# Feed-forward by block products: own buffers for the weights back, two weight sums in place, and 1/rms after the first plain products

## The chip, the cores and the metric

One Trainium2 chip, one core of it. The time is the device time of one execution in microseconds (us), the median of several runs. Below, "the trace" is the record of one profiled execution; all instants in it are us from the start of its span.

The engines are named as in the profile: PE is the matrix engine, DVE the vector engine, ACT the scalar engine, POOL the GpSimd engine, SP the engine that issues most loads. SBUF is the memory on the chip, PSUM the banks that PE writes into.

## What is computed

The program runs two blocks of two layers each, over 512 tokens of width 1024. The change concerns the feed-forward part of the second block alone, which is called once in each of its two layers (l = 0, 1):

```
def rms_norm_2(x, g): ...          # x / sqrt(mean(x*x) + eps) * g
def conv_glu_ffn(x, w_up, conv_w, conv_b, w_down):
    h = x @ w_up                                   # 1024 -> 2 * 2816
    a, b = h[..., :D_FF], h[..., D_FF:]
    ap = jnp.pad(a, ((0, 0), (CONV_WIDTH - 1, 0), (0, 0)))
    conv = conv_b + ap[:, 0:S] * conv_w[0]
    for j in range(1, CONV_WIDTH):
        conv = conv + ap[:, j:j + S] * conv_w[j]
    return (jax.nn.silu(conv) * b) @ w_down        # 2816 -> 1024
...
    x = x + conv_glu_ffn(rms_norm_2(x, norm2_g), w_up, conv_w, conv_b, w_down)
```

After the last layer the result is normalised once more (`final_norm_g`).

## The kernel before

**Layout.** x lies transposed: 8 tiles `x[k]` of 128 features by 512 tokens. Every fp32 product is made of three fp32r products: a number is split into a rounded part `hi` and a rest `lo` (on ACT a cast, on DVE a subtraction), and hi·hi + hi·lo + lo·hi is summed in PSUM. All matmuls have one line, L165; the tiles' names tell them apart. The weights come in pieces of 1 MB (`w_up`, 8 x 256 columns) or 0.5 MB (`w_down`, 4 x 256).

**Buffers.** A tile is taken by a tag and a number of buffers; a tile that is taken when all buffers of its tag are in use waits until the oldest is free. `raw()` (L249) has two buffers in the pool `wp`, and so have `whi` and `wlo`, the two parts of a split weight. `wget` loads into `raw` and splits at once (ACT L261, DVE L262). Before, `w_up` and `w_down` both go through `wget` or the same tag, so their pieces take the two `raw` buffers in turn.

**Feed-forward, `ffn2` (L1860).** The 22 tiles of hidden features are 11 pairs, each pair with a half `a` (convolved, then silu: `conv`) and a half `b` (`gate`). The first two pairs (`NPLAIN`), so four calls of `up`, are plain products: `plain` (L1777) multiplies 8 k-tiles by the two halves of the tokens, 96 matmuls of 256 columns each call. The other nine pairs go by block products, `strassen` (L1827): a 2 by 2 block product in the Winograd form with seven products of 12 matmuls of 256 columns, 84 in all. One such call, here a **step**, yields two tiles of 128 features. There are 18 steps a layer, 36 in all. Its seven weight operands come from `strassen_weights` (L1790): three are blocks of the weight itself (split on ACT L1798 and DVE L1799), four are sums of blocks, made on POOL (L1804 to L1807, s3, s1, s2, s4, into `sraw`) and split by ACT L1809 and DVE L1810 into `shi`, `slo`. The operands on the other side are blocks of h (`ha`, `hb`) and four sums of them (`ht`).

The products with `w_down` of the chunk of pairs before (24 matmuls of 512 columns, `down`) follow one to a step, two to a step in the last chunk. The last of the seven products is put off behind them (`settle`).

**The start of it.** At the end of the mixer ahead, `rms` (L325 on) makes for each half of the tokens the sum of squares (ACT L337, DVE and POOL L339), sums it over the partitions by a matmul into `n`, and takes 1/rms from it by ACT L393 and a Newton step on DVE (L394 to L396), into `r`. Only then does `halved` make h = x·gain·r, split, half of the tiles by POOL L1726 and ACT L1728, half by DVE L1734. A generator, `sums`, adds the four token sums of one k after every plain call: POOL L1747 (x·r, twice), ACT L1749, POOL L1755 to L1758, and splits.

**The end of it.** The last two tiles' product runs segment by segment, followed by the next norm or, in the last layer, by `last_rows` (L1970), which writes the result out.

**Order.** Nothing here is ordered by hand. A scheduler with a model of the engines' times puts all instructions of an engine in one fixed order; each engine works its list off in that order, and waits where an operand or a buffer isn't there yet.

Of the kernel before, what the change touches and what calls it, by code (L numbers as in the profile page):

```python
# [8 lines left out]
F32 = mybir.dt.float32  # L9
F32R = mybir.dt.float32r  # L10
I32 = mybir.dt.int32
AF = mybir.ActivationFunctionType
# [4 lines left out]
P = 128  # L17
# [132 lines left out]
class Kern:  # L150
# [1553 lines left out]
    def halved(self, x, r, scale, bias, fp, gtag, gbufs):  # L1704
# [4 lines left out]
        B = [[[None] * 4 for _ in range(2)] for _ in range(2)]  # L1709
        for k in range(KD):  # L1710
            j, kk = k // 4, k % 4
            hs = [self.t(fp, [P, S if j else H], F32R, "hb" if j else "ha", 8) for _ in range(2)]
            B[j][0][kk] = [h[:, 0:H] for h in hs]
            if j:
                B[1][1][kk] = [h[:, H:S] for h in hs]
            else:
                both = self.t(fp, [P, S], F32R, gtag, gbufs)
                B[0][1][kk] = [both[:, 0:H], both[:, H:S]]
        T = [[self.t(fp, [P, 4, H], F32R, "ht", 8) for _ in range(2)] for _ in range(4)]
        for n in range(2):  # L1720
            c = slice(n * H, (n + 1) * H)
            for k in range(KD):
                hi, lo = B[k // 4][n][k % 4]
                v = self.small(H)
                if k % 2:
                    nc.gpsimd.tensor_tensor(v, x[k][:, c], r[:, c], op=OP.mult)  # L1726
                    if bias is None:
                        nc.scalar.activation(v, v, AF.Copy, scale=scale(k))  # L1728
                    else:
                        nc.scalar.activation(v, v, AF.Identity, scale=scale(k), bias=bias(k))  # L1730
                    nc.scalar.copy(hi, v)
                    nc.vector.tensor_tensor(lo, v, hi.bitcast(F32), op=OP.subtract)
                else:
                    nc.vector.scalar_tensor_tensor(v, x[k][:, c], scale(k), r[:, c], op0=OP.mult, op1=OP.mult)  # L1734
                    if bias is None:
                        nc.scalar.copy(hi, v)
                        nc.vector.tensor_tensor(lo, v, hi.bitcast(F32), op=OP.subtract)
                    else:
                        nc.scalar.activation(hi, v, AF.Identity, bias=bias(k))
                        nc.vector.scalar_tensor_tensor(lo, v, bias(k), hi.bitcast(F32), op0=OP.add, op1=OP.subtract)  # L1740

        def sums():
            for kk in range(4):
                u = []
                for k in (kk, kk + 4):
                    u.append(self.tmp(S))
                    nc.gpsimd.tensor_tensor(u[-1], x[k], r, op=OP.mult)  # L1747
                    if bias is None:
                        nc.scalar.activation(u[-1], u[-1], AF.Copy, scale=scale(k))  # L1749
                    else:  # L1750
                        nc.scalar.activation(u[-1], u[-1], AF.Identity, scale=scale(k), bias=bias(k))
# [7 lines left out]
                hi, lo = T[kk]  # L1759
# [8 lines left out]
        return B, T, sums()  # L1768

    def strassen_setup(self, B, T, fp):  # L1770
        self.sB, self.sT = B, T
        self.sraw = self.t(fp, [P, 4, 512], F32, "sraw", 1)
        self.shi = self.t(fp, [P, 5, 512], F32R, "shi", 1)
        self.slo = self.t(fp, [P, 5, 512], F32R, "slo", 1)
        self.fp, self.owed, self.odd = fp, None, 0

    def plain(self, ws, n=2):  # L1777
# [12 lines left out]
    def strassen_weights(self, ap2d, c0):  # L1790
# [269 lines left out]
```

## Time and profile before

| | |
|---|---|
| median of 3 runs | 3638.54 us (3634.24 to 3639.56) |
| the profiled execution | 3637.94 us, its span 3636.2 us |
| granted PE clock, mean | 0.979 of full |
| PE busy | 3435.1 us, 94% |
| DVE busy | 2501.4 us, 69% |
| ACT busy | 1483.0 us, 41% |
| POOL busy | 1038.3 us, 29% |
| loads from memory | 120 GB/s over the span |

Busy shares are means over the whole program. The feed-forward of the second block begins at 2537 in layer 0 and at 3230 in layer 1; its two starts and the steps inside it are looked at by themselves below.

### The profile page before, as it was taken

Reading aid. Unit: us, or ns where it says so; the run is one execution under the profiler, and the core shown is the slowest. Engines: PE = TensorE matmul, PEld = TensorE weight load, DVE = VectorE, ACT = ScalarE, POOL = GpSimd, SP = SyncE. Lnnn points to the kernel's source line nnn. Section 1 sums busy time; section 2 is a strip of 40 time slices with the busy share of each in tenths; the row PEclk is TensorE's granted clock in tenths of the full one; section 3 lists DMA queues with packets and bytes.
Section 4 is the critical chain, followed back from the end, with each engine's and each line's share of the span. In section 5 each row is a group of like instructions: output and inputs, shape, how many; then the busy total and the mean of one; then the engine's idle time right before and its main releaser. Section 6 shows DMA issues by size and latency. Waiting matters only on the chain.

```text
span 3636.2 us, 51011 instructions
## 1 busy us (share of the span) xinstructions
PE 3435.1 (94%) x19782; PEld 2929.3 (81%) x19782; DVE 2501.4 (69%) x4093; ACT 1483.0 (41%) x2377; POOL 1038.3 (29%) x976
## 2 busy tenths in 40 slices
PE   7998999999999989999999999989999999989998
PEld 5887788888888878878887887766888877769887
DVE  5457866468786675565767557896867769787666
ACT  4233544242222243365443333335543443454444
POOL 2242322310000023212311003652534227444441
PEclk9999999999999999999999999999999999999999
DMA  6377553413333324754423324352132352513222
GB/s 220 117 238 185 145 134 107 138 59 118 104 120 112 110 95 131 240 129 130 143 87 120 122 81 127 111 166 78 57 103 88 96 160 82 174 36 99 94 87 85
DMA packets 358610, 438.79 MB, mean 121 GB/s; under 512 B 41343, under 2 KB 310289, under 8 KB 358369
## 3 DMA queue, kind: packets, MB, share of 16 engines
q1 hardware_dynamic: 327648, 345.48, 31.8%
q0 software_dynamic: 19200, 71.17, 5.6%
q10 hardware_dynamic: 11520, 18.89, 1.7%
q8 instruction: 156, 2.56, 0.3%
q14 instruction: 86, 0.70, 0.1%
HBM read 363.78 MB, written 71.70 MB: 120 GB/s over the span
## 4 chain that ended last, share of the span: by engine, by line
PE 51%; DVE 13%; DMA 5%; issue 4%; POOL 4%; ACT 2%; SPq 0%; DVEq 0%; ACTq 0%; POOLq 0%
PE d L165 25%; PE s L165 18%; PE n L165 4%; DMA raw<-in__w_up 3%; POOL sraw L1807 2%; DVE wlo L262 1%; DVE wlo L1799 1%; POOL sraw L1805 1%; PE o L165 1%; DVE sc L1394 1%; POOL sraw L1806 1%; PE g L165 1%; DVE m L1393 1%; ACT shi L1809 1%; PE d L178 1%
## 5 line engine op out<-in xcount | busy, mean ns | idle before, releaser
L261 ACT CAST whi<-raw 128x2048 fp32r<-128x2048 f32 (+2 forms) x235 | 353.4, 1504 | 487.6 <-PE s L165 247.3
L165 PE MATMUL s<-h,whi 128*128 128x256 f32 (+3 forms) x2176 | 528.6, 335 | 12.3 <-ACT whi L261 6.5
L262 DVE TENSOR_TENSOR wlo<-raw,whi 128x2048 fp32r<-128x2048 f32 (+2 forms) x219 | 405.4, 1851 | 182.8 <-ACT whi L261 182.0
L165 PE MATMUL d<-h,whi 128*128 128x512 f32 (+2 forms) x1456 | 451.8, 392 | 16.4 <-DVE h L1272 6.1
L165 PEld LDWEIGHTS s<-h,whi 128*128 128x128 f32 (+1 forms) x2176 | 370.9, 190 | 59.0 <-ACT whi L261 6.8
L165 PE MATMUL d<-g,whi 128*128 128x512 f32 (+1 forms) x1328 | 369.2, 365 | 6.1 <-DVE x L1071 2.3
L165 PE MATMUL s<-h,wlo 128*128 128x256 f32 (+3 forms) x1088 | 362.2, 334 | 2.3 <-DVE wlo L262 2.3
L165 PEld LDWEIGHTS d<-h,whi 128*128 128x128 f32 (+1 forms) x1456 | 272.1, 192 | 84.7 <-DVE h L1272 8.9
L165 PE MATMUL d<-h,wlo 128*128 128x512 f32 (+2 forms) x728 | 283.1, 392 | 1.3 <-DVE wlo L262 1.3
L165 PEld LDWEIGHTS d<-g,whi 128*128 128x128 f32 x1328 | 234.2, 188 | 49.1 <-issue 2.8
L165 PE MATMUL d<-g,wlo 128*128 128x512 f32 (+1 forms) x664 | 238.3, 364 | 0.5 <-DVE wlo L262 0.5
L165 PEld LDWEIGHTS s<-h,wlo 128*128 128x128 f32 (+1 forms) x1088 | 206.4, 190 | 24.4 <-DVE wlo L262 3.1
L165 PE MATMUL n<-h,whi 128*128 128x512 f32 (+1 forms) x768 | 217.8, 367 | 4.3 <-ACT tmp L976 2.8
L1810 DVE TENSOR_TENSOR slo<-sraw,shi 128x1024 fp32r<-128x1024 f32 x72 | 94.7, 1315 | 137.8 <-ACT shi L1809 137.8
L620 ACT ACTIVATE e<-s,sm 128x768 f32<-128x768 f32 (+1 forms) x160 | 130.9, 819 | 116.6 <-DVE sm L618 88.9
L339 POOL TENSOR_TENSOR small<-small,tmp 128x256 f32<-128x256 f32 x36 | 28.3, 786 | 521.2 <-ACT tmp L337 496.1
L165 PE MATMUL s<-ku,ku 96*128 96x512 f32 (+3 forms) x720 | 155.1, 346 | 19.0 <-ACT e L620 16.1
L618 DVE TENSOR_REDUCE sm<-s 128x1 f32<-128x768 f32 (+1 forms) x160 | 134.0, 844 | 52.5 <-PE s L165 50.9
L165 PE MATMUL s<-g,whi 128*128 128x256 f32 (+1 forms) x688 | 168.2, 335 | 0.0
L165 PEld LDWEIGHTS d<-h,wlo 128*128 128x128 f32 (+1 forms) x728 | 139.8, 192 | 31.6 <-DVE wlo L262 1.8
L165 PE MATMUL d<-ht,shi 128*128 128x256 f32 x864 | 158.7, 283 | 0.0
L1804 POOL TENSOR_TENSOR sraw<-raw 128x512 f32<-128x512 f32 x36 | 54.9, 1526 | 360.0 <-DMA raw<-in__w_up 292.1
(536 smaller groups left out, 8601.0 us busy)
## 6 DMA issues: line engine op xcount, KB each, us to landing
raw<-in__w_up SPq DMA_DIRECT2D x88, 1024.0 KB, 5.1
raw<-in__w_in SPq DMA_DIRECT2D x53, 1024.0 KB, 5.4
raw<-in__w_down SPq DMA_DIRECT2D x80, 512.0 KB, 3.5
araw<-in__w_ada SPq DMA_DIRECT2D x28, 1024.0 KB, 5.2
raw<-in__w_out SPq DMA_DIRECT2D x16, 1024.0 KB, 5.4
raw<-in__w_ada SPq DMA_DIRECT2D x15, 1024.0 KB, 9.4
U<-qd SPq DMA_DIRECT2D x32, 256.0 KB, 4.5
qd<-hl POOLq DMA_DIRECT2D x14, 512.0 KB, 4.4
```

Of the source, the lines that this page charges most:

```text
L165: self.last = self.nc.tensor.matmul(*a, **k)
L178: return self.nc.tensor.transpose(*a, **k)
L261: self.nc.scalar.copy(hi, raw[:, 0:n])
L262: (self.nc.gpsimd if self.wpool else self.nc.vector).tensor_tensor(lo, raw[:, 0:n], hi.bitcast(F32), op=OP.subtract)
L618: nc.vector.tensor_reduce(m[:, 0:1], s, axis=AX.X, op=OP.max, negate=True)
L620: nc.scalar.activation(e, s, AF.Exp, bias=m[:, 0:1], accum_out=m[:, 1:2])
L1393: nc.vector.max(m8[t], sc[t])
L1394: nc.vector.match_replace(sc[t], m8[t], sc[t], TAKEN)
L1799: nc.vector.tensor_tensor(v(lo), v(rv), v(hi).bitcast(F32), op=OP.subtract)
L1804: nc.gpsimd.tensor_tensor(s3, blk(rv, 0, 0), blk(rv, 1, 0), op=OP.add)
L1807: nc.gpsimd.tensor_tensor(s4, s2, blk(rv, 0, 1), op=OP.add)
L1810: nc.vector.tensor_tensor(self.slo[:, d, :], self.sraw[:, c, :], self.shi[:, d, :].bitcast(F32), op=OP.subtract)
```

## The change

Three things change, all in `ffn2` and what it calls.

1. **Own buffers for the weights back.** `down` takes tags `draw`, `dhi`, `dlo`, one buffer each, in the pool `fp`. `raw`, `whi` and `wlo` are left to `w_up`. To make room, `sraw` shrinks from 4 x 512 to 2 x 512, `row` becomes one of the five `tmp` tiles, `uu` one of the three `small` ones, and the last layer's output tile and `gb` take `draw` and `ya`.
2. **Two weight sums in place.** s3 and s1 still go to `sraw`. s2 and s4 overwrite the blocks a21 and a22 of `raw` itself. The four sums are split in three pieces (1024, 512, 512 columns) where there were two of 1024.
3. **First plain products without 1/rms.** `fB`, the operand of the four plain calls, is x·gain alone, split by ACT L1726 and DVE in one operation each. It lies in `dhi`, `dlo`, four `g` tiles and quarters of `shi`, `slo`, which aren't needed yet. `scaled_conv` multiplies the product by r before the convolution (DVE), and multiplies the silu's result by r on POOL (L1871), which stands for the r of the gate half. The operands of the steps (`ha`, `hb`, `ht`) are made with r by `steps`, one k after each plain call.

The diff, cut to its core:

```diff
-    def halved(self, x, r, scale, bias, fp, gtag, gbufs):
+    def strassen_setup(self, x, r, gain, fp):
...
+        self.sraw = self.t(fp, [P, 2, 512], F32, "sraw", 1)
+        self.shi = self.t(fp, [P, 5, 512], F32R, "shi", 1)
+        self.slo = self.t(fp, [P, 5, 512], F32R, "slo", 1)
+        quarter = lambda t, i: t[:, i // 2, H * (i % 2):H * (i % 2) + H]
+        first = [self.t(fp, [P, 1024], F32R, tag, 1) for tag in ("dhi", "dlo")]
+        self.fB = [[[[t[:, k * H:(k + 1) * H] for t in first] for k in range(4)], []], [[], []]]
+        for k in range(4):
+            both = self.t(fp, [P, S], F32R, "g", 12)
+            self.fB[0][1].append([both[:, 0:H], both[:, H:S]])
+            self.fB[1][0].append([quarter(t, 6 + k) for t in (self.shi, self.slo)])
+            self.fB[1][1].append([quarter(t, 2 + k) for t in (self.shi, self.slo)])
         for n in range(2):
             c = slice(n * H, (n + 1) * H)
             for k in range(KD):
-                hi, lo = B[k // 4][n][k % 4]
-                v = self.small(H)
-                if k % 2:
-                    nc.gpsimd.tensor_tensor(v, x[k][:, c], r[:, c], op=OP.mult)
...
-                else:
-                    nc.vector.scalar_tensor_tensor(v, x[k][:, c], scale(k), r[:, c], op0=OP.mult, op1=OP.mult)
...
+                hi, lo = self.fB[k // 4][n][k % 4]
+                nc.scalar.activation(hi, x[k][:, c], AF.Copy, scale=gain[:, k:k + 1])
+                nc.vector.scalar_tensor_tensor(lo, x[k][:, c], gain[:, k:k + 1], hi.bitcast(F32), op0=OP.mult, op1=OP.subtract)
...
+                for (hi, lo), v in ((ha[kk], b11), (hb[kk], u[1])):
+                    nc.scalar.copy(hi, v)
+                    nc.vector.tensor_tensor(lo, v, hi.bitcast(F32), op=OP.subtract)
...
-                    bh, bl = self.sB[k // 4][t][k % 4]
+                    bh, bl = self.fB[k // 4][t][k % 4]
...
-        s2, s4, s3, s1 = [sv(self.sraw, i) for i in (o, 1 - o, 2, 3)]
-        nc.gpsimd.tensor_tensor(s3, blk(rv, 0, 0), blk(rv, 1, 0), op=OP.add)
-        nc.gpsimd.tensor_tensor(s1, blk(rv, 1, 0), blk(rv, 1, 1), op=OP.add)
+        s3, s1 = [sv(self.sraw, i) for i in range(2)]
+        s2, s4 = blk(rv, 1, 0), blk(rv, 1, 1)
+        nc.gpsimd.tensor_tensor(s3, blk(rv, 0, 0), s2, op=OP.add)
+        nc.gpsimd.tensor_tensor(s1, s2, s4, op=OP.add)
         nc.gpsimd.tensor_tensor(s2, s1, blk(rv, 0, 0), op=OP.add)
         nc.gpsimd.tensor_tensor(s4, s2, blk(rv, 0, 1), op=OP.add)
-        for c, d in ((slice(2, 4), slice(3, 5)), (slice(0, 2), slice(1 - o, 3 - o))):
...
+        for d, v in ((slice(3, 5), flat(self.sraw)), (slice(1, 2), s2), (slice(2 - 2 * o, 3 - 2 * o), s4)):
+            sh, sl = [flat(t[:, d, :]) for t in (self.shi, self.slo)]
+            nc.scalar.copy(sh, v)
+            nc.vector.tensor_tensor(sl, v, sh.bitcast(F32), op=OP.subtract)
...
-        row = lambda: self.t(self.fp, [P, S], F32, "row", 3)
+        row = lambda: self.tmp(S)
...
+            def scaled_conv(f, ps):
+                u = self.tmp(S)
+                nc.vector.tensor_tensor(u, ps, r, op=OP.mult)
+                conv(f, u)
+                nc.gpsimd.tensor_tensor(ya[f], ya[f], r, op=OP.mult)
...
-            def down(f0, nk, g):
-                w = self.wget(a["w_down_2"][l], f0 * P, nk, g * 256, 256)
+            def down(f0, g):
+                raw = self.wload(self.t(fp, [P, 1024], F32, "draw", 1), a["w_down_2"][l], f0 * P, 4, g * 256, 256)
+                hi, lo = [self.t(fp, [P, 1024], F32R, tag, 1) for tag in ("dhi", "dlo")]
+                nc.scalar.copy(hi, raw)
+                nc.vector.tensor_tensor(lo, raw, hi.bitcast(F32), op=OP.subtract)
...
-                gb = self.t(fp, [P, S], F32, "row", 3)
+                gb = self.t(fp, [P, S], F32, "ya", 2)
...
-                o = self.sraw.rearrange("p a n -> p (a n)")[:, t * D:(t + 1) * D]
+                o = self.sraw.rearrange("p a n -> p (a n)") if t else self.t(pool, [P, D], F32, "draw", 1)
```

The diff doesn't tell how the scheduler orders the engines now. Three places, first before, then after the change; a row is a line, an operation, output<-inputs and a shape, and the last number of a name tells one buffer use from another.

SP's loads during the steps of layer 1, before:

```order
L266 DMA raw_3986_24847<-in__w_up_2 128x8x256
L266 DMA raw_3997_24949<-in__w_down_2 128x4x256
L266 DMA raw_4006_25006<-in__w_up_2 128x8x256
L266 DMA raw_4017_25108<-in__w_down_2 128x4x256
L266 DMA raw_4024_25165<-in__w_up_2 128x8x256
L266 DMA raw_4035_25267<-in__w_down_2 128x4x256
```

The same, now:

```order
L266 DMA raw_3996_25024<-in__w_up_2 128x8x256
L266 DMA draw_3987_24967<-in__w_down_2 128x4x256
L266 DMA raw_4014_25185<-in__w_up_2 128x8x256
L266 DMA draw_4007_25128<-in__w_down_2 128x4x256
L266 DMA raw_4034_25346<-in__w_up_2 128x8x256
L266 DMA draw_4025_25289<-in__w_down_2 128x4x256
```

Before, a step's `w_up` and its `w_down` load follow one another (numbers 25006, 25108, then 25165), in one tag. Now a `w_up` load stands ahead of the `w_down` load of the step before it (25185 ahead of 25128), and the two kinds have tags of their own.

ACT from the mixer's end in layer 0, before (the weight's cast, the first half's 1/rms, squares of the second half, the second half's 1/rms, first h):

```order
L261 CAST whi_3704_22386<-raw_3703_22384 128x2048
L393 ACT_TABLE_LOAD
L393 ACTIVATE r2_19216<-n_3625_22040,eps_75 128x256
L337 ACTIVATE small_3634_22111<-x_3364_21080 128x256
L337 ACTIVATE small_3635_22112<-x_3365_21081 128x256
L337 ACTIVATE tmp_3641_22130<-x_3371_21087 128x256
L393 ACTIVATE r2_19216<-n_3643_22134,eps_75 128x256
L1728 ACTIVATE small_3674_22181<-small_3674_22181,cols20_2787_17493 128x256
L1736 CAST ha_3645_22149<-small_3673_22177 128x256
```

Now, the first six rows from the same weight cast:

```order
L261 CAST whi_3692_22358<-raw_3691_22356 128x2048
L393 ACT_TABLE_LOAD
L393 ACTIVATE r2_19216<-n_3625_22040,eps_75 128x256
L1726 ACTIVATE dhi_3648_22152<-x_3364_21080,cols20_2787_17493 128x256
L1726 ACTIVATE dhi_3648_22152<-x_3365_21081,cols20_2787_17493 128x256
L1726 ACTIVATE dhi_3648_22152<-x_3366_21082,cols20_2787_17493 128x256
```

and the rows 15 to 23 after that cast:

```order
L1726 ACTIVATE shi_3646_22150<-x_3368_21084,cols20_2787_17493 128x256
L337 ACTIVATE small_3634_22111<-x_3364_21080 128x256
L337 ACTIVATE small_3635_22112<-x_3365_21081 128x256
L1726 ACTIVATE shi_3646_22150<-x_3369_21085,cols20_2787_17493 128x256
L1726 ACTIVATE shi_3646_22150<-x_3370_21086,cols20_2787_17493 128x256
L1726 ACTIVATE shi_3646_22150<-x_3371_21087,cols20_2787_17493 128x256
L337 ACTIVATE tmp_3641_22130<-x_3371_21087 128x256
L393 ACTIVATE r2_19216<-n_3643_22134,eps_75 128x256
L1857 ACTIVATE ya_3684_22320<-tmp_3683_22318,cols20_2787_17493,colsw20_2790_17503 128x512
```

Before, the first operand of PE (`ha`) is written behind the second half's 1/rms. Now `dhi` is written behind the first half's, and the second half's squares and 1/rms stand behind 13 to 17 casts of x·gain.

POOL from the second half's 1/rms in layer 0, before:

```order
L339 TENSOR_TENSOR small_3635_22112<-small_3635_22112,tmp_3640_22127 128x256
L339 TENSOR_TENSOR small_3635_22112<-small_3635_22112,tmp_3641_22130 128x256
L1726 TENSOR_TENSOR small_3674_22181<-x_3365_21081,r2_19216 128x256
L1747 TENSOR_TENSOR tmp_3699_22366<-x_3364_21080,r2_19216 128x512
L1747 TENSOR_TENSOR tmp_3700_22369<-x_3368_21084,r2_19216 128x512
L1726 TENSOR_TENSOR small_3676_22190<-x_3367_21083,r2_19216 128x256
L1755 TENSOR_TENSOR tmp_3701_22372<-tmp_3699_22366 128x256
L1726 TENSOR_TENSOR small_3678_22199<-x_3369_21085,r2_19216 128x256
L1756 TENSOR_TENSOR tmp_3701_22372<-tmp_3700_22369,tmp_3699_22366 128x256
L1757 TENSOR_TENSOR tmp_3702_22373<-tmp_3700_22369,tmp_3701_22372 128x256
```

and now:

```order
L339 TENSOR_TENSOR small_3635_22112<-small_3635_22112,tmp_3640_22127 128x256
L339 TENSOR_TENSOR small_3635_22112<-small_3635_22112,tmp_3641_22130 128x256
L1738 TENSOR_TENSOR tmp_3687_22334<-x_3364_21080,r2_19216 128x512
L1738 TENSOR_TENSOR tmp_3688_22337<-x_3368_21084,r2_19216 128x512
L1743 TENSOR_TENSOR tmp_3689_22340<-tmp_3687_22334 128x256
L1871 TENSOR_TENSOR ya_3684_22320<-ya_3684_22320,r2_19216 128x512
L1744 TENSOR_TENSOR tmp_3689_22340<-tmp_3688_22337,tmp_3687_22334 128x256
L1745 TENSOR_TENSOR tmp_3690_22341<-tmp_3688_22337,tmp_3689_22340 128x256
L1738 TENSOR_TENSOR tmp_3700_22470<-x_3365_21081,r2_19216 128x512
L1738 TENSOR_TENSOR tmp_3701_22473<-x_3369_21085,r2_19216 128x512
L1871 TENSOR_TENSOR ya_3686_22328<-ya_3686_22328,r2_19216 128x512
L1746 TENSOR_TENSOR tmp_3690_22341<-tmp_3690_22341,tmp_3688_22337 128x256
```

Before, POOL makes h for the plain products (L1726) among the token sums. Now L1726 of POOL is gone, each pair of `x·r` (L1738) feeds `ha` and `hb` too, the products `ya·r` (L1871, four in all) are new, and the first step's weight sums (L1788 on) come in between the token sums.

## Rows read from the trace of the kernel before

**Rows 1.** Windows, start of the feed-forward in layers 0, 1: us, length, busy (count) by engine, PE clock.

```profile
2537.40:2618.30 80.90, 67.03 (x487) 63.89 (x486) 68.82 (x78) 46.24 (x78) 51.30 (x44) 0.89 0.17 53
3229.80:3309.40 79.60, 66.14 (x494) 62.54 (x493) 70.27 (x79) 46.53 (x80) 52.91 (x44) 0.94 0.17 56
```

**Rows 2.** Chain of waits through one step, 2700 to 2722: start us, us, what.

```profile
2703.37 5.11 DMA raw<-in__w_up
...
2708.62 0.04 POOL sraw L1804
2710.25 1.75 POOL sraw L1805
2712.06 1.30 POOL sraw L1806
2713.43 2.17 POOL sraw L1807
2715.63 1.06 ACT shi L1809
...
2719.74 0.61 DVE wlo L1799
...
2720.40 5.17 DMA raw<-in__w_up
```

**Rows 3.** Timeline of PE: first matmul of a step (start us, us, what, [idle before <-releaser]).

```profile
2666.25 0.39 PE L165 MATMUL d<-ha,whi 128*128 128x256 f32 x1 [0.70 <-ACT whi L1798]
2871.32 0.39 PE L165 MATMUL d<-ha,whi 128*128 128x256 f32 x1 [0.24 <-ACT whi L1798]
3356.66 0.39 PE L165 MATMUL d<-ha,whi 128*128 128x256 f32 x1 [0.47 <-ACT whi L1798]
3563.29 0.39 PE L165 MATMUL d<-ha,whi 128*128 128x256 f32 x1 [0.55 <-ACT whi L1798]
3309.40 0.28 PE L165 MATMUL d<-ha,whi 128*128 128x256 f32 x1
3324.94 0.28 PE L165 MATMUL d<-ha,whi 128*128 128x256 f32 x1
```

**Rows 4.** Waits of PE from 2668 to 2890: what for, us in total, times, longest.

```profile
PE d L165 <- DVE wlo L1799: 5.4, 13, 0.4
PE d L165 <- ACT whi L1798: 5.3, 12, 0.8
```

**Rows 5.** Groups by line, POOL, 2700 to 2862: xcount | busy us, mean ns | idle before.

```profile
L1804 POOL TENSOR_TENSOR sraw<-raw 128x512 f32<-128x512 f32 x9 | 13.7, 1526 | 90.9 <-DMA raw<-in__w_up 90.9
```

**Rows 6.** Windows, one step of layer 0: us, length, busy by engine in Rows 1's order.

```profile
2700.90:2718.00 17.10, 16.25 (x109) 14.55 (x109) 11.80 (x18) 6.38 (x10) 6.82 (x4) 1.00 0.29 93
```

**Rows 7.** Timeline of PE, from mixer to first plain product, layers 0 and 1.

```profile
2537.05 0.47 PE L165 MATMUL d<-mix,wlo 128*128 128x256 f32 x1
2544.40 2.08 PE L165 MATMUL n<-small,ones 128*128 128x256 f32 x4 [6.88 <-DVE small L339]
2548.32 0.58 PE L165 MATMUL d<-ha,whi 128*128 128x256 f32 x1 [1.85 <-ACT ha L1736]
...
3239.62 0.80 PE L165 MATMUL d<-ha,whi 128*128 128x256 f32 x2 [2.42 <-ACT ha L1736]
```

**Rows 8.** Timeline of ACT, layer 0: 1/rms of the first half of the tokens.

```profile
2540.45 0.47 ACT L393 ACTIVATE r<-n,eps 128x256 f32<-128x256 f32 x1
```

**Rows 9.** Timeline of DVE, layer 0: end of 1/rms, second half, and first h.

```profile
2548.20 0.42 DVE L396 SCALAR_TENSOR_TENSOR r<-small,r 128x256 f32<-128x256 f32 x1
...
2548.95 1.50 DVE L1734 SCALAR_TENSOR_TENSOR small<-x,cols,r 128x256 f32<-128x256 f32 x1
```

**Rows 10.** Groups by line, POOL, 2546 to 2588 (token sums of layer 0).

```profile
L1747 POOL TENSOR_TENSOR tmp<-x,r 128x512 f32<-128x512 f32 x8 | 12.2, 1536 | 1.4 <-DVE r L396 1.4
...
L1758 POOL TENSOR_TENSOR tmp<-tmp,tmp 128x256 f32<-128x256 f32 x4 | 5.8, 1451 | 0.1
...
L1755 POOL TENSOR_TENSOR tmp<-tmp 128x256 f32<-128x256 f32 x4 | 3.5, 873 | 0.0
```

More of the change, by code (lines that the diff above doesn't have):

```diff
@@ L1701, in mixer2 @@
         return x
-    def halved(self, x, r, scale, bias, fp, gtag, gbufs):
+    def strassen_setup(self, x, r, gain, fp):
         nc = self.nc
         H = S // 2
[L1709 to L1715, printed above, removed]
-            else:
-                both = self.t(fp, [P, S], F32R, gtag, gbufs)
-                B[0][1][kk] = [both[:, 0:H], both[:, H:S]]
-        T = [[self.t(fp, [P, 4, H], F32R, "ht", 8) for _ in range(2)] for _ in range(4)]
+        self.fp, self.owed, self.odd = fp, None, 0
+        self.sraw = self.t(fp, [P, 2, 512], F32, "sraw", 1)
[9 more added lines that the diff above has]
+            self.fB[1][1].append([quarter(t, 2 + k) for t in (self.shi, self.slo)])
         for n in range(2):
@@ L1722, in halved, with steps @@
             for k in range(KD):
-                hi, lo = B[k // 4][n][k % 4]
-                v = self.small(H)
-                if k % 2:
-                    nc.gpsimd.tensor_tensor(v, x[k][:, c], r[:, c], op=OP.mult)
[L1727 to L1733, printed above, removed]
-                    nc.vector.scalar_tensor_tensor(v, x[k][:, c], scale(k), r[:, c], op0=OP.mult, op1=OP.mult)
[L1735 to L1742, printed above, removed]
+                hi, lo = self.fB[k // 4][n][k % 4]
+                nc.scalar.activation(hi, x[k][:, c], AF.Copy, scale=gain[:, k:k + 1])
+                nc.vector.scalar_tensor_tensor(lo, x[k][:, c], gain[:, k:k + 1], hi.bitcast(F32), op0=OP.mult, op1=OP.subtract)
+        ha = [[self.t(fp, [P, H], F32R, "ha", 8) for _ in range(2)] for _ in range(4)]
+        hb = [[self.t(fp, [P, S], F32R, "hb", 8) for _ in range(2)] for _ in range(4)]
+        self.sB = [[ha], [[[p[:, n * H:(n + 1) * H] for p in q] for q in hb] for n in range(2)]]
+        self.sT = [[self.t(fp, [P, 4, H], F32R, "ht", 8) for _ in range(2)] for _ in range(4)]
+        def steps():
             for kk in range(4):
@@ L1747, in sums @@
                     nc.gpsimd.tensor_tensor(u[-1], x[k], r, op=OP.mult)
[L1748 to L1751, printed above, removed]
+                    nc.scalar.activation(u[-1], u[-1], AF.Copy, scale=gain[:, k:k + 1])
                 b11, b12, b21, b22 = u[0][:, 0:H], u[0][:, H:S], u[1][:, 0:H], u[1][:, H:S]
@@ L1766, in sums @@
                 yield
[L1768 to L1775, printed above, removed]
+        return steps()
     def plain(self, ws, n=2):
@@ L1841, in strassen @@
         self.settle()
-        r1, u2, pc, pdd, pf = row(), self.t(self.fp, [P, H], F32, "uu", 2), bank(), bank(), bank()
+        r1, u2, pc, pdd, pf = row(), self.small(H), bank(), bank(), bank()
         self.block_product(pc, w["s3"], t(1))
@@ L1863, in ffn2 @@
             fp = self.pool(es, "fp", self.other())
-            gain = col["norm2"]
-            B, T, sums = self.halved(x, self.r2, lambda k: gain[:, k:k + 1], None, fp, "g", 12)
-            self.strassen_setup(B, T, fp)
+            r = self.r2
+            steps = self.strassen_setup(x, r, col["norm2"], fp)
             (w0, w1, w2), cb = self.cw, col["conv_b"]
@@ L1885, in up @@
                     for j, ps in enumerate(self.plain([(w, 0), (w, 1)])):
-                        use(2 * p0 + j, ps)
-                    next(sums, None)
+                        plain_use(2 * p0 + j, ps)
+                    next(steps, None)
                 else:
@@ L1890, in up @@
                     self.strassen(w, lambda j, row: use(2 * p0 + j, row))
-            def down(f0, nk, g):
-                w = self.wget(a["w_down_2"][l], f0 * P, nk, g * 256, 256)
+            def down(f0, g):
[3 more added lines that the diff above has]
+                nc.vector.tensor_tensor(lo, raw, hi.bitcast(F32), op=OP.subtract)
+                w = [v.rearrange("p (k n) -> p k n", k=4) for v in (hi, lo)]
                 for j in range(2):
@@ L1896, in down @@
                     ps = self.pd()
-                    self.dense(w, j * P, P, gt, f0, nk, S, ps)
+                    self.dense(w, j * P, P, gt, f0, 4, S, ps)
                     nc.vector.tensor_tensor(x[m], ps, x[m], op=OP.add)
@@ L1904, in ffn2 @@
                 for p0 in range(f0 // 2, f0 // 2 + npair):
-                    for c0, use in ((p0 * 256, conv), (F + p0 * 256, gate)):
-                        up(p0, c0, use)
+                    for c0, use, plain_use in ((p0 * 256, conv, scaled_conv), (F + p0 * 256, gate, gate)):
+                        up(p0, c0, use, plain_use)
                         for _ in range(per):
@@ L1909, in ffn2 @@
                             self.settle()
-                todo = [lambda f=f0, g=g: down(f, 4, g) for g in range(4)]
+                todo = [lambda f=f0, g=g: down(f, g) for g in range(4)]
                 f0 += 2 * npair
```

7 lines of the change are left out of this document (3 added, 4 removed).

## The prediction

> **What bounds the kernel now.** PE is busy 94% of the span, so at first sight it is bound by PE. I looked for stretches of the feed-forward where it isn't, in four views: windows, the timeline of PE, the chain of waits, and the groups of POOL.
>
> The timeline of PE gives the length of a step. Where nothing stalls, one step follows another after 3324.94 − 3309.40 = 15.54 us [rows 3]: this is what 84 matmuls of 256 columns and 24 of 512 take at full clock. In the middle of layer 0 the step starts at 2666.25 and 2871.32 lie 12 steps apart, which is 17.09 us each; in layer 1, 3356.66 and 3563.29 lie 12 apart, 17.22 each. Each of the four starts shows PE waiting for ACT's part of the split weight. So 24 of the 36 steps lose 1.55 to 1.68 us. The waits under their own name come to 5.4 + 5.3 = 10.7 us for 12 steps [rows 4], 0.9 a step; the rest hides in matmul rows that read longer around the waits.
>
> The chain of waits tells why [rows 2]. It is a loop that never touches PE: load of w_up 5.11 us, four sums on POOL (1.63 with its gap, 1.75, 1.30, 2.17), cast on ACT 1.06, splits on DVE to the last one (0.61), and only then the next load, 2720.40 − 2703.37 = 17.03 us after the first. Of two `raw` buffers w_down always holds one, so w_up has one left, and a step's load can't start before the last reader of the load ahead. POOL agrees: in nine steps it stands idle 90.9 us for that load [rows 5], 10 us a step. Nothing is short of capacity: in one step of 17.10 us DVE is busy 11.80, ACT 6.38, POOL 6.82 [rows 6]. This is a latency loop through one buffer.
>
> The second place is the start of the feed-forward. From the mixer's end to the second step's start pass 80.90 us in layer 0 and 79.60 in layer 1, with PE busy 67.03 and 66.14 [rows 1], partly below full clock (0.89 and 0.94 of it granted). In layer 0 PE stops behind 2537.05 for the squares (6.88 idle) and again for the first h (1.85), which it has at 2548.32 [rows 7].
>
> **The change, part by part.**
>
> *Own buffers for w_down.* w_up has both `raw` buffers, and its load moves ahead on SP by one place. A buffer's own round now is load 5.11, sums 6.8, three splits of at most 1.1 on ACT and as much on DVE: some 17 to 19 us against two steps, 31.1. The loop falls below PE's 15.54, and PE becomes the bound: 12 × (17.09 − 15.54) = 18.6 in layer 0, 12 × (17.22 − 15.54) = 20.2 in layer 1, and 1.5 for the steps around these. Some irregularity will stay; I take 0.15 us for each of 30 steps, 4.5. So −35. From below: a third of the loss may come back as waits for other single buffers (−25). From above: nothing is left (−40).
>
> *What this loads on others.* On SP a w_down load now stands behind a w_up load that waits for its buffer. It is needed only two thirds into its step, and its `dhi`, single, is free when the step before has used it: about 7 us of slack by the order (60 matmuls of 256 columns stand ahead of it in its step); a miss would cost at most a half-size load, under 5.11 [rows 2]. I cost it at nothing.
>
> *In-place sums.* They cost no operation more on POOL. s4 overwrites a22 and so must wait for a22's split on DVE, which stands half a step ahead of it; and `raw` is held until s2 and s4 are split, which the buffer's round above contains. The third split adds one ACT and one DVE instruction a step, less than 0.61 each, on engines that have 9 and 4 us to spare [rows 6]. Nothing.
>
> *`row`, `uu`, `gb`, the output tile in other tags.* The same operations; `gb` waits for a `ya` tile and has the last chunk's products as cover, without which it would cost less than a load, 5.1. Nothing.
>
> *The start.* First h no longer needs 1/rms. ACT has the first half's r done at 2540.9 [rows 8]; x·gain follows at once, and DVE's rest, so PE starts at about 2541.5 instead of 2548.32. But the second half's squares and r stand behind 13 to 17 casts of some 0.45 on ACT: r, complete at 2548.6 before [rows 9], comes some 7 us later, at 2555.5. From there POOL is the path. Until the first step is complete it must do 8 products x·r of 1.54, 16 sums at the middle of 1.45 and 0.87 [rows 10], 4 products ya·r (as x·r, 1.54), and the weight sums of two steps, 2 × 6.8: 12.3 + 18.6 + 6.2 + 13.7 = 50.8. With 4 us of idle between them it ends at 2610, and 3 us of split and last products follow: the second step starts at 2613 where it started at 2618.3. So −5 a layer, −10 in all. Best end: r comes only 3 us late and POOL never idles, −13 a layer; PE's own work would even be done earlier. Worst end: the dearest rows throughout, 16 × 1.45 and 8 weight sums of 2.17, so 12.3 + 23.2 + 6.2 + 17.4 = 59.1 and an end at 2622, +4 a layer.
>
> A row that speaks against this part: a DVE operation of 256 columns takes 0.42 us, and 1.50 when it starts beside a running POOL operation [rows 9], while sums of one shape on POOL take 0.87 to 1.45 [rows 10]. The two engines hinder one another. The Trainium skill (page "SBUF — State Buffer", section "SBUF: two separate sides") says why: a DVE operation with two SBUF inputs and a GpSimd operation that reads SBUF share a port pair as an exclusive lock, and whichever starts second fully blocks. The trace agrees as far as these rows go; by that rule the start would come out at its worst end, since DVE now reads products from SBUF in the convolution, and the sum would be 3612 instead of 3594.
>
> **Sum.** 3637.9 (span 3636.2 and 1.7 around it) − 35 − 10 = 3593; the median of the runs stands 0.6 above the profiled execution: 3594.
>
> **Rivals.**
>
> *A, the start gives nothing or loses.* POOL and DVE take turns, POOL's path grows to 59 us, and the second step starts at 2618 to 2622. For it: [rows 9, 10]. Against it: 6.9 us of products leave POOL there, and PE starts 7 us earlier. Time: 3638.5 − 35 + 0 to 9 = 3603 to 3612.
>
> *B, the loop stays.* Something else than the buffer, such as the order on DVE or `sraw`, holds the next load back, and only the start gains: 3628. Against it: the load follows the last split within 0.1 us [rows 2], and the order now puts it a step ahead.
>
> *C, slower.* With the load early, POOL's sums fall beside DVE's longest operations. If the two never run side by side, a step takes 11.80 + 6.82 = 18.6 us [rows 6] and that is the new loop: 24 × (18.6 − 17.15) = 35 more, 3673. It decides once less than 1.5 us a step can overlap. Against it: in the same step of 17.10 they overlap by at least that much already, and both sums contain time spent waiting.
>
> *D, all of it.* Both parts at their best ends: 3573.
>
> **Chances.** Forecast 0.62, A 0.20, D 0.06, B 0.06, C 0.06. A measurement of this kernel can tell about 0.2%, 7.3 us. Forecast, A and D are faster, and a third of B: 0.90. The rest of B, where the start gains less than its ten, is no change: 0.04. C is slower: 0.06. The range 3574 to 3614 holds forecast and A with their bounds and leaves out B, C and D.
>
> **What would show it.** Right: steps of 15.5 to 15.8 us all through, no waits of PE for ACT's or DVE's part of the weight, the w_up load issued a step ahead of its POOL sums, POOL's idle time no longer ended by that load; the first plain product about 4 us behind the mixer's last, and 75 us from there to the second step. Wrong: steps still near 17 with POOL waiting for the load (B), steps above 17 with POOL and DVE rows stretched (C), or an early first product but a second step 80 us or later behind the mixer (A).

## The result, and the profile after

The changed kernel takes 3594.48 us (median of 4 runs, 3593.96 to 3604.56), the kernel before, beside it, 3636.43 (median of 4, 3634.24 to 3639.56): a ratio of 0.9891, 95% interval 0.9871 to 0.991. The forecast was 3594. The total came out as forecast, but two of its terms did not: the loop and the tail behind it gave more than was counted, and the start gave nothing. The rest of this document is about that.

The profiled execution of the changed kernel took 3594.06 us, its span 3592.3, 43.9 less than before. The timeline of PE shows where (start us, us, what; line by line: the mixer's last product, the first plain product, the first matmul of the first, second, 8th and 17th step; in layer 1 the mixer's last product, second and 17th step):

```profile
2537.78 0.47 PE L165 MATMUL d<-mix,wlo 128*128 128x256 f32 x1
...
2542.10 0.38 PE L165 MATMUL d<-dhi,whi 128*128 128x256 f32 x1 [3.85 <-ACT dhi L1726]
...
2589.99 0.28 PE L165 MATMUL d<-ha,whi 128*128 128x256 f32 x1
...
2618.76 0.28 PE L165 MATMUL d<-ha,whi 128*128 128x256 f32 x1
...
2713.74 0.28 PE L165 MATMUL d<-ha,whi 128*128 128x256 f32 x1
...
2852.46 0.28 PE L165 MATMUL d<-ha,whi 128*128 128x256 f32 x1
...
3205.19 0.28 PE L165 MATMUL d<-mix,wlo 128*128 128x256 f32 x1
...
3288.78 0.28 PE L165 MATMUL d<-ha,whi 128*128 128x256 f32 x1
...
3522.19 0.28 PE L165 MATMUL d<-ha,whi 128*128 128x256 f32 x1
```

Cut at these points, and at the same points of the kernel before (2537.05, 2618.26, 2871.32, 3230.47, 3309.40, 3563.29 in its timeline of PE; [rows 3, 7] show most of them), the span divides so:

| stretch | before, us | after, us | difference |
|---|---|---|---|
| up to the mixer's last product, layer 0 | 2537.05 | 2537.78 | +0.7 |
| from there to the second step | 81.21 | 80.98 | −0.2 |
| second to 17th step | 253.06 | 233.70 | −19.4 |
| 17th step to the mixer's last product, layer 1 | 359.16 | 352.73 | −6.4 |
| from there to the second step | 78.93 | 83.59 | +4.7 |
| second to 17th step | 253.89 | 233.41 | −20.5 |
| 17th step to the end | 72.91 | 70.11 | −2.8 |

One thing shifts a little between two rows. The put-off product of a step (12 matmuls of 256 columns, 1.4 us) came behind the first matmul of the next step before, and from the 6th step of layer 0 and the 4th of layer 1 on it comes ahead of it now: from the second to the 17th step PE has 1631 and 1634 matmuls in its timeline, before 1620 and 1619. For equal work the loop gave 1.4 us more in each layer than these rows say, and the stretch behind the 17th step 1.4 less.

**The loop is gone.** From the 8th to the 17th step, 138.72 us for nine steps are 15.41 us each. The chain of waits of the changed kernel between 2700 and 2732, which before ran over the load, POOL, ACT and DVE [rows 2], is one line (start us, us, what):

```profile
2699.89 32.11 PE d L165 x227
```

The timeline of SP shows the loads of w_up and w_down in turn, 7.6 to 7.9 us apart, w_up every 15.4, while before a w_up load came 17.03 behind the last:

```profile
2707.11 0.37 SPq L266 DMA_DIRECT2D raw<-in__w_up  x1
2714.67 0.37 SPq L266 DMA_DIRECT2D draw<-in__w_down  x1
2722.47 0.37 SPq L266 DMA_DIRECT2D raw<-in__w_up  x1
2730.32 0.37 SPq L266 DMA_DIRECT2D draw<-in__w_down  x1
```

Ahead of its first sum of a step (its line is now L1788; group of lines, 2684 to 2846, busy, mean ns, idle before and its releaser) POOL still stands idle, 90.8 us in 11 steps where [rows 5] has 90.9 in nine, but the load no longer ends it. DVE does, by freeing `sraw`:

```profile
L1788 POOL TENSOR_TENSOR sraw<-raw 128x512 f32<-128x512 f32 x11 | 18.5, 1682 | 90.8 <-DVE slo L1796 90.8
```

**The start is no shorter.** PE has its first plain product at 2542.10, 4.3 us behind the mixer's last, and gets through the four plain calls without a stop; the first step begins 52 us behind the mixer instead of 67 (at 2589.99, before at 2604.16). Then it takes 28.8 us, where it took 14.1. The waits of PE from 2538 to 2618.7 tell for what (us in total, times, longest):

```profile
PE d L165 <- DVE ha L1749: 4.5, 2, 2.7
PE d L165 <- ACT ha L1748: 4.3, 1, 4.3
PE d L165 <- ACT dhi L1726: 3.9, 1, 3.9
PE d L165 <- DVE hb L1749: 1.5, 1, 1.5
```

The one for `dhi` stands ahead of the first plain product; the other three are for the splits of the operands of the first step. The windows of the two starts (us, length, busy by engine in the order PE, PEld (weight loads), DVE, ACT, POOL, then PE clock, DMA share and GB/s) answer to [rows 1], and the stretch from 2560 to 2612, with the steady steps under it, shows which engine is full:

```profile
2538.10:2618.70 80.60, 66.37 (x486) 63.81 (x485) 74.60 (x81) 46.87 (x80) 56.08 (x41) 0.89 0.20 66
3205.50:3288.70 83.20, 67.26 (x482) 64.06 (x483) 72.77 (x80) 46.60 (x80) 54.15 (x40) 0.88 0.20 64
```

```profile
2560.00:2612.00 52.00, 43.24 (x323) 41.82 (x322) 50.38 (x42) 28.69 (x48) 47.66 (x33) 0.87 0.16 52
2684.00:2846.00 162.00, 162.00 (x1147) 152.44 (x1146) 129.01 (x180) 78.72 (x119) 70.89 (x41) 1.00 0.31 101
```

Between 2560 and 2612 DVE is busy 50.38 us of 52.00, POOL 47.66. In the steady steps DVE is busy 129 of 162 us and POOL 71.

The chain of waits through the start (2538 to 2622; start us, us, what) says which of the two holds PE back. From 2563 to 2582.8 it runs over POOL, and from 2583.2 to 2614.3 over DVE, which is busy 30.9 of these 31.0 us (issue is time that the profile gives to no wait):

```profile
2582.03 0.75 POOL tmp L1746
2582.78 0.02 issue
2582.80 0.41 ACT ht L1753
2583.21 0.02 issue
2583.24 1.26 DVE ht L1754
...
2613.10 1.14 DVE hb L1749
2614.25 0.04 issue
2614.29 1.24 PE d L165 x7
```

In layer 1 it is the same: DVE is the chain from 3253.7 to 3284.9, but for 0.8 us of ACT.

### The profile page after: what moved, and what is told of

It reads as the page before. It is cut to its first block, busy times and chain, and to the rows that moved or that the text cites. A ratio compares the mean times of both kernels' runs of the same rounds, so it can differ in the third digit from the quotient of the medians.

```text
span 3592.3 us, 51055 instructions
## 1 busy us (share of the span) xinstructions
PE 3416.2 (95%) x19782; PEld 2930.7 (82%) x19782; DVE 2522.5 (70%) x4137; ACT 1497.7 (42%) x2415; POOL 1052.7 (29%) x968
## 4 chain that ended last, share of the span: by engine, by line
PE 62%; DVE 11%; issue 3%; ACT 2%; POOL 1%; DMA 1%; SPq 0%; DVEq 0%; ACTq 0%; POOLq 0%
PE d L165 36%; PE s L165 19%; PE n L165 4%; DVE wlo L262 1%; DVE sc L1394 1%; PE o L165 1%; DVE m L1393 1%; PE g L165 1%; PE d L178 1%; PE b L178 1%; DVE wlo L1783 1%; ACT whi L261 1%; DVE hl L369 1%; DVE slo L1796 0%; DVE pt L1555 0%
## 5 line engine op out<-in xcount | busy, mean ns | idle before, releaser
L261 ACT CAST whi<-raw 128x2048 fp32r<-128x2048 f32 (+2 forms) x195 | 311.3, 1597 | 466.4 <-PE s L165 249.0
L262 DVE TENSOR_TENSOR wlo<-raw,whi 128x2048 fp32r<-128x2048 f32 (+3 forms) x179 | 358.1, 2001 | 183.2 <-ACT whi L261 182.5
L165 PE MATMUL d<-g,dhi 128*128 128x512 f32 x640 | 197.7, 391 | 0.1
L165 PE MATMUL d<-g,whi 128*128 128x256 f32 (+1 forms) x688 | 167.3, 337 | 6.1 <-DVE x L1071 2.3
L165 PEld LDWEIGHTS n<-h,whi 128*128 128x128 f32 x768 | 135.6, 192 | 26.8 <-ACT tmp L976 4.0
L165 PEld LDWEIGHTS s<-ku,ku 96*128 96x128 f32 (+1 forms) x720 | 120.5, 190 | 41.5 <-ACT e L620 18.5
L165 PE MATMUL d<-whi,h 128*128 128x256 f32 x768 | 149.0, 289 | 0.0
```

The costliest lines, as they stand in the source:

```text
L165: self.last = self.nc.tensor.matmul(*a, **k)
L261: self.nc.scalar.copy(hi, raw[:, 0:n])
L262: (self.nc.gpsimd if self.wpool else self.nc.vector).tensor_tensor(lo, raw[:, 0:n], hi.bitcast(F32), op=OP.subtract)
```

## The experiments

Twelve runs of ten kernels, in three lots; each lot shared the runs of the kernel before (3641.0, 3638.3 and 3638.7 us, medians), so ratios compare across lots, and times within one. "Behind the mixer" is the time from the mixer's last product in PE's timeline. It tells more than the medians do: the stretch ahead of that product, which is no part of any edit here, ended at 2543.5 us in one run of `loop_alone` and at 2536.7 in the other.

**The change without the new start (loop_alone).** `halved` of the kernel before comes back, and `plain` reads `sB`:

```diff
-            steps = self.strassen_setup(x, r, col["norm2"], fp)
+            B, T, steps = self.halved(x, self.r2, lambda k: gain[:, k:k + 1], None, fp, "g", 12)
+            self.strassen_setup(B, T, fp)
...
-                    bh, bl = self.fB[k // 4][t][k % 4]
+                    bh, bl = self.sB[k // 4][t][k % 4]
...
-                    for c0, use, plain_use in ((p0 * 256, conv, scaled_conv), (F + p0 * 256, gate, gate)):
+                    for c0, use, plain_use in ((p0 * 256, conv, conv), (F + p0 * 256, gate, gate)):
```

> The change without its third part: w_down has its own buffers and s2, s4 are made in place, but the start of the feed-forward is that of the kernel before (h with 1/rms for the plain products). Theory (the loop through one raw buffer was the whole gain, and the new start costs what POOL and DVE lose to one another): steps of 15.4 us all through, no waits of PE on the split weight, and the second step not later behind the mixer than in the kernel before (81 and 79 us), so 3583 to 3592, faster than the changed kernel. Rival (the forecast's term: the new start gains 5 us a layer): 3599 to 3606, slower than the changed kernel.

Measured: 3595.83 us (3593.05 to 3599.14), ratio 0.9876 (0.9861 to 0.9891). All steps take 15.4 us. The second step comes 84.1 and 83.5 us behind the mixer, so 2.9 and 4.6 later than before, where the expectation said not later; 1.4 of it is the put-off product, which stands ahead of this step here. The other 1.5 and 3.2 us come with the first two parts of the change, since the start is the old one. No step after it loses anything; the 17th comes 315.3 and 314.7 behind the mixer, in the changed kernel 314.7 and 317.0. The theory held in that the new start is worth nothing here; that the kernel would be faster than the changed one did not come true. The time itself lies 4 us above the range given, where the rival began 3 us higher; 5.7 us more than in the changed kernel lie ahead of the mixer's last product in its trace.

**The new start alone (start_alone).** w_down goes through `wget` again, and the four sums into a `sraw` of 4 x 512:

```diff
-        self.sraw = self.t(fp, [P, 2, 512], F32, "sraw", 1)
+        self.sraw = self.t(fp, [P, 4, 512], F32, "sraw", 1)
...
-                raw = self.wload(self.t(fp, [P, 1024], F32, "draw", 1), a["w_down_2"][l], f0 * P, 4, g * 256, 256)
...
+                w = self.wget(a["w_down_2"][l], f0 * P, 4, g * 256, 256)
```

> The third part alone: plain products without 1/rms, while w_down shares raw, whi and wlo with w_up and the four weight sums go to a buffer of their own. Theory: the loop of 17.0 to 17.2 us a step is back, with POOL idle 9 to 10 us a step for the load of w_up, and the start gives nothing: 3634 to 3643, no change from the kernel before. Rival (the start gains by itself): 3624 to 3629.

Measured: 3636.97 us (3634.05 to 3642.07), ratio 0.9989 (0.9979 to 0.9998). The steps are back at 17.0 us, and POOL's first sum (group of lines, 2700 to 2862) waits for the load, as in [rows 5]:

```profile
L1787 POOL TENSOR_TENSOR sraw<-raw 128x512 f32<-128x512 f32 x9 | 14.1, 1564 | 91.3 <-DMA raw<-in__w_up 80.4 <-DVE tmp L1823 10.9
```

The second step comes 79.6 and 82.5 us behind the mixer, 1.6 earlier and 3.6 later than before, and the 17th 332.5 and 335.1; before, 334.3 and 332.8. So the new start alone gives nothing either, as the theory said. The 4 us by which the runs are below those of before (the interval ends just under 1) aren't found in this stretch, and are under what one measurement can tell.

**One line undone: w_down loads into `raw` (down_in_raw).**

```diff
-                raw = self.wload(self.t(fp, [P, 1024], F32, "draw", 1), a["w_down_2"][l], f0 * P, 4, g * 256, 256)
+                raw = self.wload(self.raw(), a["w_down_2"][l], f0 * P, 4, g * 256, 256)[:, 0:1024]
```

> The changed kernel with one line undone: the load of w_down goes into the raw buffers that w_up uses; its split parts keep their own buffers, the sums stay in place. Theory (one raw buffer for w_up makes the loop): the next load of w_up waits for the last split of the sums made in raw, so a step is as long as before or longer, 17 to 18.5 us, and the time 3630 to 3665. Rival (the shared whi and wlo, or the order, made the loop): steps stay at 15.4 to 15.7 and the time at 3594 to 3600.

Measured: 3674.55 us (3670.47 to 3678.26), ratio 1.0092 (1.0076 to 1.0107), slower than the kernel before, and above the range given. The timeline of PE has its 5th and 17th step here (12 steps, 17.82 us each, by turns 14 and 22), and SP's loads of one kind stand some 18 us apart again:

```profile
2669.20 0.28 PE L165 MATMUL d<-ha,whi 128*128 128x256 f32 x1
...
2883.09 0.28 PE L165 MATMUL d<-ha,whi 128*128 128x256 f32 x1
```

```profile
2751.51 0.37 SPq L266 DMA_DIRECT2D raw<-in__w_down  x1
2757.75 0.37 SPq L266 DMA_DIRECT2D raw<-in__w_up  x1
2769.42 0.37 SPq L266 DMA_DIRECT2D raw<-in__w_down  x1
2776.34 0.37 SPq L266 DMA_DIRECT2D raw<-in__w_up  x1
```

POOL waits for the load (group of lines, 2688 to 2890):

```profile
L1788 POOL TENSOR_TENSOR sraw<-raw 128x512 f32<-128x512 f32 x11 | 14.3, 1298 | 116.6 <-DMA raw<-in__w_up 116.6
```

What SP's loads wait for (2688 to 2890: us, times, longest) are readers of `raw`, w_down's split and that of the sums made in place:

```profile
SPq L266 <- DVE dlo L1887: 121.8, 11, 11.2
SPq L266 <- DVE slo L1796: 68.1, 11, 6.5
```

So the shared buffer is enough to make the loop, with the split parts in buffers of their own. The scheduler's order was free to follow the line and wasn't held fixed. That a step is longer than before (17.8 for 17.1 us) fits with `raw` being held now until the sums made in it are split, for which the loads wait here; in-place sums weren't tried by themselves.

**1/rms earlier (rms_early).** ACT's order at the start by hand:

```diff
+                with self.tc.issue_after(self.nr_ins if n else self.sq_ins):
                     nc.scalar.activation(hi, x[k][:, c], AF.Copy, scale=gain[:, k:k + 1])
```

(`sq_ins` is the last square of the second half, `nr_ins` its 1/rms on ACT.)

> The changed kernel with ACT's order set by hand at the start: the squares of the second half of the tokens before the casts of x times gain, and its 1/rms before the casts of the second half. 1/rms is complete some 5 to 7 us earlier, PE's first plain product about 1 us later. Theory (from 1/rms on, DVE and POOL both work without a gap, so what starts them earlier ends them earlier): the second step comes 4 to 7 us earlier in each layer, 3581 to 3588. Rival (DVE has no time to spare before 1/rms either, the work is only moved): 3592 to 3596.

Measured: 3598.83 us (3596.9 to 3601.82), ratio 0.9885 (0.987 to 0.9899): nothing gained, so the theory falls. 1/rms was complete at 2551.8, 14.3 us behind the mixer instead of 17.5, which is 3.2 earlier where 5 to 7 were expected; PE's first product came about 2 later where 1 was expected, and the second step 82.5 and 84.8 behind the mixer. What was won went into a wait of POOL further down its list (waits of POOL, 2540 to 2620: us, times, longest), for the silu's result which `ya·r` reads:

```profile
POOL ya L1873 <- ACT ya L1862: 8.5, 1, 8.5
...
POOL tmp L1740 <- DVE r L397: 6.5, 1, 6.5
```

In the changed kernel that wait for the silu's result is 2.6 us.

**What the products with r cost.** Three kernels: `ya·r` left out (no_ya_r), `ya·r` on DVE (ya_r_on_dve), `ps·r` left out (no_u_r):

```diff
-                nc.gpsimd.tensor_tensor(ya[f], ya[f], r, op=OP.mult)
```

> The changed kernel without the four products of the silu's result with r on POOL (they are left out, so the gate half has no 1/rms in the first four tiles). Theory D (DVE is the one that is never free between 1/rms and the second step): POOL gets 7 us of room, DVE only what its rows were stretched by it, and the second step comes 1 to 4 us earlier in layer 0. Theory P (POOL's list, which also waits there for the silu, sets the end): 7 to 10 us earlier, 71 to 74 us behind the mixer where it was 81.

Measured: 3591.88 us (3589.36 to 3596.71), ratio 0.9867 (0.9853 to 0.9882). The second step comes 79.9 and 82.4 us behind the mixer, 1.1 and 1.2 earlier. This is theory D's size; theory P, that POOL's list sets the end, falls.

```diff
-                nc.gpsimd.tensor_tensor(ya[f], ya[f], r, op=OP.mult)
+                nc.vector.tensor_tensor(ya[f], ya[f], r, op=OP.mult)
```

> The changed kernel with the four products ya times r on DVE in place of POOL. Theory D: DVE has 3 to 5 us more to do, so the second step comes 0 to 4 us later in layer 0, 81 to 85 us behind the mixer, and the time stays or rises by up to 8. Theory P: 5 to 9 us earlier, 72 to 76, and the time falls by 10 or more.

Measured: 3595.19 us (3591.5 to 3600.61), ratio 0.9876 (0.9861 to 0.9891). The second step comes 80.5 and 81.7 us behind the mixer, 0.4 and 1.9 earlier, and the 17th comes 313.2 and 314.3 behind the mixer, 1.5 and 2.7 earlier. Neither theory said that: DVE with more to do is no later, and POOL with less to do doesn't set the end.

```diff
-                u = self.tmp(S)
-                nc.vector.tensor_tensor(u, ps, r, op=OP.mult)
-                conv(f, u)
+                conv(f, ps)
```

> The changed kernel without the four products of the plain result with r on DVE (left out: the convolution half of the first four tiles has no 1/rms and is read from PSUM as in the kernel before). Theory D: DVE has 2.7 us less, and its convolutions no longer read two tiles of SBUF beside POOL, so the second step comes 3 to 7 us earlier. Theory P: ya is ready earlier for POOL, which takes away its wait of 2.6 us for it; 0 to 3 us earlier.

Measured: 3591.36 us (3590.46 to 3592.49), ratio 0.9864 (0.985 to 0.9879). The second step: 81.2 us behind the mixer in layer 0, no earlier, and 76.5 in layer 1, 7.1 earlier. In layer 0 DVE stood 3.8 us for ACT's cast of a plain weight, which the scheduler had put elsewhere; so this decides for D in one layer and nothing in the other.

**Both together (early_and_dve).** ACT's order of rms_early, and `ya·r` on DVE:

> 1/rms early by ACT's order, as in rms_early, and ya times r on DVE, so that POOL's list no longer stands still for the silu (8.5 us in rms_early). Theory P: the second step comes 7 to 12 us earlier than in the changed kernel, 69 to 74 us behind the mixer in layer 0, and the time falls by 14 to 24. Theory D: 79 to 84 us, the time stays within 6.

Measured: 3596.17 us (3596.14 to 3596.53), ratio 0.9878 (0.9861 to 0.9894). The second step comes 81.4 and 82.8 us behind the mixer. This is theory D: with POOL free of the wait, the start still ends where it did.

**On one chip, once more (changed_again, loop_alone_again, ya_r_on_dve_again).** The changed kernel, the one without the new start, and the one with `ya·r` on DVE:

> The changed kernel itself, on the chip and beside the runs that the two below are compared with: 0.987 to 0.990 of the kernel before. The step's 15.41 us and the start's 81 and 83.6 us behind the mixer should come again to 0.5 us.

> The change without the new start, once more on the same chip as the changed kernel. If the new start is worth nothing (theory), the two stand within 5 us of each other. If it is worth the 10 us of the forecast, this one is 7 to 13 us slower.

> ya times r on DVE in place of POOL, once more beside the changed kernel. From its trace (the 17th step 1.5 and 2.7 us earlier behind the mixer) it should be 2 to 6 us faster than the changed kernel; if that was chance, within 2 us.

Measured: 3596.51 (3594.28 to 3597.6), 3593.80 (3590.48 to 3595.45) and 3591.15 us (3590.94 to 3593.81); ratios 0.9884 (0.9869 to 0.9899), 0.9876 (0.9861 to 0.9891) and 0.987 (0.9853 to 0.9886). The steps of the changed kernel take 15.41 us again, and the second step comes 80.9 and 82.6 us behind the mixer: 0.1 and 1.0 earlier than in its first run, where the expectation allowed 0.5. So a difference of 1 us in layer 1, as in no_ya_r, tells nothing. Without the new start the kernel's median is 2.7 us lower, less than a measurement can tell: the new start is worth nothing that could be measured. `ya·r` on DVE is 5.4 us faster than the changed kernel here, as its trace let expect, but their intervals overlap, and in the lot before its median was 4 us higher; that it is faster isn't shown. In its second trace the 17th step comes 313.0 and 314.7 behind the mixer, 1.6 and 1.3 earlier than in the changed kernel's.

**No x·r on POOL (no_x_r).**

```diff
-                    nc.gpsimd.tensor_tensor(u[-1], x[k], r, op=OP.mult)
-                    nc.scalar.activation(u[-1], u[-1], AF.Copy, scale=gain[:, k:k + 1])
+                    nc.scalar.activation(u[-1], x[k], AF.Copy, scale=gain[:, k:k + 1])
```

> The changed kernel without the eight products x times r on POOL: ACT makes gain times x from x itself, so the operands of the steps have no 1/rms (left out). POOL has 12 us less in the start and need not wait for 1/rms. Theory T (DVE is never free there because a third of its time goes to rows that wait beside POOL): the second step comes 8 to 14 us earlier in each layer, 67 to 73 and 70 to 76 us behind the mixer, and the time falls by 15 to 28. Rival (the start is held by something else, such as PE's own list, ACT, or the weights' loads): 0 to 4 us earlier a layer, and 0 to 8 in all.

Measured: 3590.68 us (3586.81 to 3594.56), ratio 0.9869 (0.9854 to 0.9883). The second step comes 76.6 and 80.6 us behind the mixer, 4.4 and 3.0 earlier: near the rival's size (0 to 4), not theory T's. With 12 us taken from POOL, which now waits (for ACT, 15.5 us), DVE is still busy 60.67 of 67.00 us (columns as above, from 0.6 to 67.6 us behind the mixer; in the changed kernel's same stretch, 61.37), and PE's waits (2538 to 2625) are for the same splits:

```profile
2545.00:2612.00 67.00, 58.29 (x443) 57.02 (x444) 60.67 (x70) 43.23 (x75) 41.96 (x31) 0.90 0.20 63
```

```profile
PE d L165 <- ACT ha L1747: 2.5, 1, 2.5
PE d L165 <- DVE ha L1748: 2.4, 1, 2.4
```

Not tried: the four sums outside `raw` together with own buffers for w_down, for which SBUF has no room.

## Why the prediction was right, and where it was not

**The loop: right in its mechanism, its size above the upper bound.** The forecast counted 38.8 us for 24 steps and took 4.5 off for irregularity; the 15 steps of each layer from the second to the 17th gave 39.8 (19.4 and 20.5). The irregularity came only right behind the start (two steps of 15.7 to 17.4 in each layer, in which 1.4 us are the put-off product, so about 1 us a layer is lost), and the other steps run at 15.41, 0.13 under the 15.54 I had taken for PE's floor from [rows 3]. The stretch from the 17th step to the end of the feed-forward, which I had given 1.5 with other steps, gave 3.5 in layer 0 (to the first operation of the next mixer, 60.4 to 56.9 us) and 2.8 with all that follows in layer 1. Together 46 where the sum had 35 and 40 for its best end. One undone line brings the loop back, so its cause is shown.

**What this loads on others: right.** No wait of PE between 2684 and 2852; in the steps w_down's loads and the in-place sums stay under cover. The start is another matter (below).

**The start: wrong.** The step that failed is "From there POOL is the path", with its end "the second step starts at 2613". Up to there the working held: PE's first product was put at 2541.5 and came at 2542.1, 1/rms at 2555.5 and came at 2555.3. POOL's list was then done at 2613.7, 4 us later than counted, but it alone did not set the end: POOL could be relieved of 12 us (no x·r) for 3 to 4 a layer, and of its four products for 1. DVE is the engine that is never free from 2560 to 2612, and the chain of waits runs over it alone for the last 31 us ahead of 2614. I had not added up DVE's list at all: rows of it that take 0.7 us elsewhere take 1.2 to 1.6 here. The measured terms are −0.2 and +4.7 in place of −5 and −5 (the prediction's 79.60 for layer 1 was read from 0.7 us ahead of the mixer's last product; the table has 78.93). Not all of this is the new start's: with the old one, the other two parts alone put the second step 1.5 and 3.2 us later for equal work. This is rival A, at a chance of 0.20: POOL's list took 58.4 us from 1/rms on, where it says 59, and the second step comes at 2618.8, in layer 1 a little past its unfavourable end. Its time, 3603 to 3612, was not reached since the loop gave more.

How the rows stretch is in DVE's groups (by shape, mean ns) of the start, 2560 to 2612:

```profile
L359 DVE TENSOR_TENSOR g<-ya,g 128x512 fp32r<-128x512 f32 x4 | 6.5, 1638 | 0.0
...
L1858 DVE SCALAR_TENSOR_TENSOR ya<-tmp,colsw,ya 128x511 f32<-128x511 f32 x3 | 3.8, 1251 | 0.0
L1859 DVE SCALAR_TENSOR_TENSOR ya<-tmp,colsw,ya 128x510 f32<-128x510 f32 x3 | 3.6, 1201 | 0.1
...
L1864 DVE TENSOR_TENSOR ya<-d,ya 128x512 f32<-128x512 f32 x4 | 2.7, 678 | 0.0
```

and of the steady steps, 2684 to 2846:

```profile
L1893 DVE TENSOR_TENSOR x<-d,x 128x512 f32<-128x512 f32 x20 | 13.6, 682 | 4.6 <-PE d L165 4.6
...
L1859 DVE SCALAR_TENSOR_TENSOR ya<-tmp,colsw,ya 128x510 f32<-128x510 f32 x12 | 8.9, 743 | 0.0
L1858 DVE SCALAR_TENSOR_TENSOR ya<-tmp,colsw,ya 128x511 f32<-128x511 f32 x12 | 8.7, 752 | 2.1 <-ACT ya L1857 2.1
L359 DVE TENSOR_TENSOR g<-ya,g 128x512 fp32r<-128x512 f32 x10 | 6.4, 683 | 0.0
```

Products that read PSUM (`x<-d,x`, `ya<-d,ya`) take 0.68 us in both. Those with both inputs in SBUF take 0.68 to 0.75 in the steps, where POOL is busy 71 of 162 us, and 1.20 to 1.64 in the start, where it is busy 48 of 52. This is what the Trainium skill states (page "SBUF — State Buffer", section "SBUF: two separate sides"): a DVE operation with two SBUF inputs and a GpSimd operation that reads SBUF exclude one another, and the one that starts second waits for the other. The trace agrees in which operations stretch. But the rule alone gave too much: taking 12 us of POOL's work away should then have brought the second step forward by about as much, and brought it 3 to 4. From 1/rms (2555.3) to the second step DVE's rows sum to 65 us; at the shortest row of each form in this trace they would take 43, so by this estimate a third of its list is stretch. Whether all of that is waiting beside POOL stays open, and so does what a shorter list on DVE would give: leaving out four of its products gave 7 us in one layer and nothing in the other.

**The total.** −40 and −6 for the loop and its tail, +4.4 for the two starts, −3 in the mixer between (why isn't shown; in the second run of the changed kernel the stretch from the 17th step to the mixer's last product is 1.3 us longer) and +0.7 ahead: −43.9. The sum of the forecast, −45, was near it because the 14 us by which the starts fell short were made up by 11 more from the loop and its tail and 3 from the mixer: that the total agreed is luck.

## What to carry to other kernels

When a load, sums and splits form a chain that ends in freeing the load's own buffer, the length of that chain, not any engine's busy share, is the period; look who else takes buffers from the same tag. Before work is moved to start earlier, add up the list of every engine that has part in it, at the durations that rows have beside their neighbours: an engine at 69% of the span can be the one that is full in the stretch that matters. And when a sum of several terms comes out right, cut the span at the same points before and after: here it was right by two errors that cancelled.

## What the runs showed of the hardware

In the changed kernel, fp32 operations on DVE with two SBUF inputs take up to 2.4 times as long in the stretch where POOL is busy nine tenths of the time (1638 ns for 683, 128 x 512), while those that read PSUM take the same (678 and 682). And an engine that could start earlier simply waited elsewhere: POOL's idle time for the silu rose from 2.6 to 8.5 us when 1/rms came 3 us earlier.
